# A second buffer for the S5 input matrix, filled one chunk ahead, in a hybrid decoder trunk

## The chip, the cores and the metric

The kernel runs on one core of a Trainium2 chip. The metric is the device time of one execution in microseconds (us); lower is better. The engines are named as in the profile: PE (TensorE, matrix products), PEld (its weight loads), DVE (VectorE), ACT (ScalarE), POOL (GpSimd) and SP (SyncE, which here only issues transfers). Each engine works through its own list of instructions, and waits on semaphores for the others.

## The reference, cut to what matters

Two layers (DEPTH = 2) over 288 columns: one prompt of 256 positions and 8 samples of 4. Everything is float32.

```python
def _layer(x, ...):
    z = x @ w_in
    u, cv, cg = z[..., :1024], z[..., 1024:2048], z[..., 2048:]
    y5, h_re, h_im = _s5(u, h0_re, h0_im, ...)        # 64 groups x 16 channels, 64 complex states
    g5 = gelu(y5);  s5_out = g5 * sigmoid(g5 @ s5_w_glu)
    c = causal_dwconv(cv * sigmoid(cg), width 31);  c = silu(_ln(c))
    x = _ln(ALPHA * x + concat([s5_out, c]) @ w_out)
    ...                                               # ConvFFN and input embedding, each with an _ln

def _s5(u, ...):
    bu = einsum(u, q * B)              # into the states; q from lam and dt
    h  = associative_scan(a, bu)       # over positions
    y  = Re(C h) + d * u
```

The product into the states (`bu`) and the one out of them (`y`) are what the change is about; the rest of the layer is most of the time.

## The kernel before

The big projections run on PE over blocks of 128 x 128 weights with 288 columns. A weight arrives as `wraw` (eight blocks, 512 KB); ACT rounds it to `whi` (L202), DVE makes the remainder `wlo` (L145, a helper through which all DVE work goes), and PE multiplies three times per block (L379, L384 or L381, L385), so a unit of eight blocks is 24 matmuls. I count PE's place in the program in such matmuls from the start of the layer's input projection, and call this its position. The first blocks of layer 0 are multiplied in float32 at once (L375).

Beside the projections of a layer's mixer runs the S5 part, in 8 chunks of 128 channels (`c` = 0 to 7), written as Python generators that a small planner advances whenever PE has been given enough work. It keeps two accounts of time, `pe_t` for what PE and `dve_c` for what DVE has been given; `wait(ns)` and `until(t)` yield until `pe_t` has passed a time, `at(ns, fn)` calls `fn` then. So the planner only sets the order of instructions on each engine. For chunk c:

- `make_e`: the rows of B are scaled by q on DVE (`s5_into`: four instructions that read `sqb`, `sbt`; "into" below) and spread by two ACT instructions under two masks into the block-diagonal `em` (L947). In layer 1 the scaled rows are made early in layer 0's feed-forward, go to memory (`se_d`) and come back as `sbt`, so there is no "into".
- `make_o`: the matrix out of the states, `om`, and the short-range matrix: DVE makes `pw` and `bsm`, PE multiplies them (`kps`, L807), ACT copies the product under masks (`kp`, L812), DVE adds d, and through memory (`k_d`) it becomes `tm`.
- `inject`: PE makes `bu` from `em` and the chunk's columns `ust` (L399, 64 matmuls). It sets `state["i"] = c`.
- `scan`: DVE turns, scans and turns back the states and writes them shifted to `hin`. POOL makes the tables for it (`stb`, L990, finished on ACT at L996).
- `tail`: PE makes `y` from `hin` with `om` and `ust` with `tm` (L399), ACT and DVE apply the gelu.

`kps`, `y` and the set-up's `tp` share one PSUM buffer (tag "one"), so the `y` of chunk c, which stands behind the `kps` of chunk c + 1 in the program, needs that `kps` read out by `kp`. `em` has one buffer: chunk c + 1's may be written once chunk c's `bu` is done, and `prep`, which makes the matrices, waits for `state["i"] >= c - 1` first. The width-31 convolution of the mixer's other half (eight parts) gives `cvo`, eight tiles.

In the set-up of layer 0, `tp` (L710) transposes q through PE; POOL stores it (`q_d`, L717) and loads it spread out as the first `sqb` (L751).

Of the kernel before, what the change touches and what calls it, by code (L numbers as in the profile page):

```python
# [7 lines left out]
F32 = mybir.dt.float32  # L8
# [5 lines left out]
P = 128  # L14
# [5 lines left out]
TOK = SEQ + NB * NT  # L20
# [5 lines left out]
S5C = 8  # L26
CVC = 8
# [15 lines left out]
NCH = TOK // STEP  # L43
# [21 lines left out]
L0_LAG = 4000.0  # L65
LOOK = 1
FREE_LAG = 500.0
EARLY_LAG = 7000.0
EARLY_RATE = 0.5
EV_GAP = 10  # L70
# [88 lines left out]
class Core:  # L159
# [46 lines left out]
    def stream_lo(self, upto):  # L206
        upto = min(upto, self.nblk // SB - 1)
        while self.next_lo <= upto:
# [8 lines left out]
            self.next_lo += 1  # L217
            self.freed.append((s + RAW_BUFS, self.dve_c + FREE_LAG))

# [25 lines left out]
    def at(self, ns, fn):  # L245

        self.timed.append((self.pe_t + ns, fn))

    def run_timed(self, force=False):
        for x in list(self.timed):  # L250
# [333 lines left out]
    def setup(self, mp):  # L584
# [34 lines left out]
        p, s = exp_parts(ld, *w)  # L619
# [7 lines left out]
        thl, t1, t2, f = tl(), tl(), tl(), tl()  # L627
# [21 lines left out]
        p, s = exp_parts(x1, *w)  # L649
# [50 lines left out]
        yield None  # L700
        for _ in range(W1):
            yield None
        tp = self.ps.tile([P, 512], F32, tag="one", name="tp", bufs=1)
        for s in range(4):
            for i in range(2):
# [108 lines left out]
    def s5_early(self, l, pool):  # L814
# [20 lines left out]
        for c in range(S5C):  # L835
            bt, qb = [self.s5_load(l, c, pool, eng, w) for w in "bq"]
            cc, bc = self.s5_load(l, c, pool, eng, "o")
            yield 1.0
            yield from self.wait(EARLY_LAG)
            m = work([P, 4, 2, ST])  # L840
            yield from self.s5_into(m, bt, qb)
            ed, od, kd = [self.dp.tile(shp, F32, tag=f"{n}_d{c}", name=f"{n}_d{c}", bufs=1) for n, shp in (
                ("se", [P, 4, 2, ST]), ("so", [P, 4, 2, 4, CIN]), ("sk", [P, 7 * 2 * CIN]))]
            yield from self.wait(EARLY_LAG)
            eng.dma_start(ed, m)
# [14 lines left out]
    def s5(self, l, mp):  # L860
# [5 lines left out]
        def once(n, shp):  # L866
            return mp.tile(shp, F32, name=n, tag=n, bufs=1)
        fin = once("fin", [P, NPAIR, 2, 9])
        h0 = once("h0", [P, NPAIR, 2, NB])
        self.sm = {"e": once("em", [P, 4, 2, P]), "o": once("om", [P, 4, 2, P])}  # L870
        em, om = self.sm["e"], self.sm["o"]
        tm = once("tm", [P, 4, P])
        pw = once("pw", [P, 4, 2, 5, CIN])
        bs = once("bsm", [P, 4, 2, 2, CIN])
# [49 lines left out]
        def load_o(c, eng):  # L924
            if early:
                o = mp.tile([P, 4, 2, 4, CIN], F32, name="sqb", tag="sqb", bufs=1)
                eng.dma_start(o, early[c][1])
                load_t(c, early[c][2])
                return (o,)
            return self.s5_load(l, c, mp, eng, "o")  # L930
# [8 lines left out]
        def make_e(c, bt, qb=None):  # L939
            m = bt  # L940
            if not early:
                m = work([P, 4, 2, ST])
                yield from self.s5_into(m, bt, qb)
            mf = m.rearrange("p q i s -> p (q i) s")
            ef = em.rearrange("p q i m -> p (q i) m")
            for g in range(2):
                nc.scalar.activation(ef[:, :, g * ST:(g + 1) * ST], mf, AF.Copy, scale=self.mask2[:, g:g + 1])  # L947

        def make_o(c, cc, bc=None):

            if early:
                pk = cc
            else:
                yield from self.s5_out(l, c, cc, bc, pw, bs, work)
                yield from self.wait(PJ_LAG)
                while state["y"]:
                    yield None
                state["k"] = True
                self.s5_steps(bs, pw, kp)
                self.at(PS_LAG + 500.0, lambda: state.update(k=False))  # L960
                yield None
                k0 = kp[:, 3].rearrange("p g o -> p (g o)")
                V.scalar_tensor_tensor(k0, self.eye, self.prm("s5_d", c), k0, op0=OP.mult, op1=OP.add)
                kd = self.dp.tile([P, 7 * 2 * CIN], F32, tag="k_d", name="k_d", bufs=2)
                G.dma_start(kd, kp.rearrange("p k g o -> p (k g o)"))
                pk = pw[:, :, :, 1:5]
            while state["p"] < c - 1:
                yield None
            of = om.rearrange("p q i (r g o) -> p (q i) r g o", g=2, o=CIN)
            pf = pk.rearrange("p q i k o -> p (q i) k o")  # L970
            for g in range(2):
                h = slice(g * ST, (g + 1) * ST)
                nc.scalar.activation(of[h, :, :, g], pf[h], AF.Copy)
            if early:
                self.at(PS_LAG, lambda: state.update(o=c))
                return

            def back():
                load_t(c, kd)
                self.at(LOAD_LAG, lambda: state.update(o=c))  # L980
            self.at(BACK_LAG, back)
# [14 lines left out]
            self.at(2500.0, lambda: nc.scalar.activation(f, tb, AF.Sin, scale=6.283185307179586 / 4294967296.0))  # L996
            return f

        def inject(us):
            v = self.ps.tile([P, 2, 512], F32, tag="two", name="bu", bufs=1)  # L1000
            self.pe_t += 1000.0
            for q in range(4):
                for i in range(2):
                    self.strips(v[:, i, q * NCH:(q + 1) * NCH], em[:, q, i], us[:, q], True, True)
            return v

        def scan(c, v, tb):
# [69 lines left out]
        state = {"i": -1, "p": -1, "e": -1, "o": -1, "y": False, "k": False}  # L1077
        finals = []

        def prep():  # L1080
            if l == 0:
                yield from self.wait(Q_LAG)
            while l and not self.u_d:
                yield None
            ge = load_e(0, nc.gpsimd, bt0)
            yield from self.wait(L0_LAG if l == 0 else LOAD_LAG)
            go = go0
            for c in range(S5C):
                while state["i"] < c - 1:
                    yield None  # L1090
                yield from make_e(c, *ge)
                state["e"] = c
                if c + 1 < S5C:
                    self.at(B_LAG, lambda: nxt.append(load_e(c + 1, nc.sync)))
                yield from make_o(c, *go)
                if c + 1 < S5C:
                    go = load_o(c + 1, nc.sync)
                    while not nxt:
                        yield None
                    ge = nxt.pop()  # L1100
                    yield from self.wait(3000.0)
            self.rate = RATE[l]

        def main():
            if l == 0:
                yield from self.wait(M0_LAG)
            G.memset(om, 0.0)
            tb = tables(0)
            initial()
            for c in range(S5C):  # L1110
                while c not in ready or state["e"] < c:
                    yield None
                self.rate = RATE[l]
                v = inject(us[c])
                state["i"] = c
                yield from self.wait(PS_LAG)
                yield from scan(c, v, tb)
                if c + 1 < S5C:
                    tb = tables(c + 1)
                streams.insert(0, tail(c, us.pop(c)))  # L1120
# [21 lines left out]
        nxt = []  # L1142
# [10 lines left out]
        us, ready = {}, set()  # L1153
# [5 lines left out]
    def mixer(self, l, ph):  # L1159
        nc, a = self.nc, self.a  # L1160
        V = self.V
        with self.tc.tile_pool(name="mx", bufs=1) as mp:
            self.u32 = [mp.tile([P, TOK], F32, name=f"u32_{c}", tag=f"u32_{c}") for c in range(S5C)]
            cvo = [mp.tile([P, TOK], F32, name=f"cvo_{c}", tag=f"cvo_{c}") for c in range(CVC)]
            self.u_d, self.gdone = {}, []
            scan = self.scan = self.start(self.s5(l, mp), 0.0)

# [472 lines left out]
```

## Time and profile before

| | us |
|---|---|
| three runs | 2725.92, 2732.58, 2732.72 (median 2732.58) |
| profiled execution | 2730.52, span 2728.7, mean granted clock 0.99 |
| busy in the span | PE 2661.9, DVE 1836.0, ACT 1353.4, POOL 331.7 |

The span runs from the first to the last instruction of the profiled execution; times in the views count from its start. Layer 0's mixer lies at about 28 to 275 us, layer 1's at about 1376 to 1640 us. In a row of the timeline the bracket gives how long the engine sat idle before that instruction, and what it waited for.

### The profile page before, as it was taken

To read this page: it belongs to the slowest core of one execution; us is meant where nothing else is said; L and a number is where in the kernel's file an instruction comes from. 1 tells how busy PE (TensorE), PEld (TensorE's weight loads), DVE (VectorE), ACT (ScalarE), POOL (GpSimd) and SP (SyncE) were. 2 spreads that over 40 slices of the span, in tenths; PEclk is the share of its full clock that TensorE was granted. 3 is DMA by queue.
4 is the path that set the end of the run, shared out by engine and by line. 5 is a ranking of instruction groups with operands and counts; after the bars stand their busy time and mean duration, and the time that the engine had idled before them with its cause. 6 is when DMAs were issued, how large, how long until landed. Compare 5 with 4: busy or idle time off the path is not lost.

```text
span 2728.7 us, 57971 instructions
## 1 busy us (share of the span) xinstructions
PE 2661.9 (98%) x23696; PEld 2603.1 (95%) x23696; DVE 1836.0 (67%) x3016; ACT 1353.4 (50%) x2224; POOL 331.7 (12%) x913
## 2 busy tenths in 40 slices
PE   8889999999999999999998999999999999999997
PEld 7888999999999999999988889999999999999997
DVE  6986767665677556667776668776546664566686
ACT  3444547553555345546464445565435553455363
POOL 3553001000001000000034420010000000000000
PEclk9999999999999999999999999999999999999998
DMA  7877544555566645554568764454545555455543
GB/s 239 241 229 224 167 151 158 169 190 190 183 197 199 200 155 170 172 167 153 165 193 236 224 196 166 158 161 157 189 159 164 161 185 167 159 162 182 163 150 102
DMA packets 188041, 487.99 MB, mean 179 GB/s; under 512 B 48416, under 2 KB 74288, under 8 KB 187520
## 3 DMA queue, kind: packets, MB, share of 16 engines
q1 hardware_dynamic: 176896, 444.27, 51.0%
q0 software_dynamic: 10880, 40.03, 5.2%
q8 instruction: 186, 3.05, 0.5%
q14 instruction: 79, 0.65, 0.1%
HBM read 463.98 MB, written 24.87 MB: 179 GB/s over the span
## 4 chain that ended last, share of the span: by engine, by line
PE 88%; DVE 3%; DMA 3%; issue 1%; ACT 1%; POOL 1%; SPq 0%; ACTq 0%; DVEq 0%; POOLq 0%
PE acc L379 28%; PE acc L384 26%; PE acc L385 26%; PE acc L361 2%; PE acc L381 2%; PE acc L1225 2%; DVE sw L145 1%; PE y L399 1%; DMA cbuf<-in_convi_dram 1%; DVE wlo L145 1%; DMA ust<-u_d 1%; DVE x L145 1%; PE bu L399 0%; PE lnp L469 0%; DMA sqb<-q_d 0%
## 5 line engine op out<-in xcount | busy, mean ns | idle before, releaser
L379 PE MATMUL acc<-xh,whi 128*128 128x288 f32 x4656 | 1378.7, 296 | 7.6 <-ACT e L1344 3.2
L385 PE MATMUL acc<-xh,wlo 128*128 128x288 f32 x4357 | 1287.7, 296 | 3.0 <-issue 3.0
L384 PE MATMUL acc<-xl,whi 128*128 128x288 f32 x4357 | 1289.0, 296 | 0.6 <-DVE xl L145 0.3
L202 ACT ACTIVATE whi<-wraw 128x1024 fp32r<-128x1024 f32 x766 | 791.6, 1051 | 331.8 <-PE acc L384 211.2
L145 DVE TENSOR_TENSOR wlo<-wraw,whi 128x1024 fp32r<-128x1024 f32 x766 | 922.9, 1227 | 31.8 <-ACT whi L202 14.3
L379 PEld LDWEIGHTS acc<-xh,whi 128*128 128x128 f32 x4656 | 879.3, 189 | 15.4 <-ACT e L1344 4.1
L385 PEld LDWEIGHTS acc<-xh,wlo 128*128 128x128 f32 x4357 | 821.8, 189 | 3.3 <-issue 3.3
L384 PEld LDWEIGHTS acc<-xl,whi 128*128 128x128 f32 x4357 | 821.9, 189 | 2.4 <-DVE xl L145 2.0
L379 PE MATMUL acc<-hh,whi 128*128 128x288 f32 x1408 | 416.3, 296 | 0.0
L145 DVE SCALAR_TENSOR_TENSOR fo<-fe,parf,fo 128x304 f32<-128x304 f32 x352 | 188.3, 535 | 323.3 <-ACT fo L1377 317.0
L385 PE MATMUL acc<-hh,wlo 128*128 128x288 f32 x1312 | 387.7, 296 | 0.0
L384 PE MATMUL acc<-hl,whi 128*128 128x288 f32 x1312 | 387.0, 295 | 0.0
L379 PEld LDWEIGHTS acc<-hh,whi 128*128 128x128 f32 x1408 | 265.1, 188 | 0.5
L384 PEld LDWEIGHTS acc<-hl,whi 128*128 128x128 f32 x1312 | 247.0, 188 | 0.0
L385 PEld LDWEIGHTS acc<-hh,wlo 128*128 128x128 f32 x1312 | 246.7, 188 | 0.0
L1373 ACT ACTIVATE fe<-acc 128x256 f32<-128x256 f32 x176 | 67.6, 384 | 287.8 <-PE acc L385 287.8
L1383 POOL COPY fstage<-fe 128x9 f32<-128x9 f32 x176 | 45.0, 256 | 1037.0 <-ACT fe L1374 1014.1
L438 ACT ACTIVATE ln_q<-x 128x288 f32<-128x288 f32 x90 | 40.2, 446 | 221.5 <-DVE x L145 221.5
L145 DVE TENSOR_TENSOR x<-x,acc 128x288 f32<-128x288 f32 x64 | 29.1, 454 | 139.3 <-PE acc L385 139.3
L1377 ACT ACTIVATE fo<-fe,parf 128x304 f32<-128x304 f32 x176 | 113.1, 643 | 16.4
L1397 ACT ACTIVATE hh<-fth 128x288 fp32r<-128x288 f32 x88 | 39.2, 446 | 163.2 <-DVE fth L145 163.2
L145 DVE SCALAR_TENSOR_TENSOR x<-x,acc 128x288 f32<-128x288 f32 x64 | 29.0, 453 | 123.8 <-PE acc L385 123.7
(251 smaller groups left out, 2389.4 us busy)
## 6 DMA issues: line engine op xcount, KB each, us to landing
wraw<-in_wts_dram SPq DMA_DIRECT2D x776, 512.0 KB
stack<-cb_d POOLq DMA_DIRECT2D x32, 282.0 KB, 6.6
big<-cb_d POOLq DMA_DIRECT2D x24, 282.0 KB, 6.7
cbuf<-in_convi_dram POOLq DMA_DIRECT2D x16, 283.5 KB, 7.3
cb_d<-cbuf POOLq DMA_DIRECT2D x16, 283.5 KB, 3.6
out_dram<-cb_d POOLq DMA_DIRECT2D x16, 283.5 KB, 8.0
sbt<-in_s5b_dram SPq DMA_DIRECT2D x15, 256.0 KB
sqb<-q_d SPq DMA_DIRECT2D x60, 64.0 KB
```

The lines of the kernel that those rows point to most:

```text
L145: return f(out, *args, **kw)
L202: self.nc.scalar.activation(hi, self.raw[s], AF.Copy)
L361: nc.tensor.matmul(out, w, xl, start=False, stop=False)
L379: nc.tensor.matmul(out, w[0], xh, start=first, stop=False)
L381: nc.tensor.matmul(out, w[1], xh, start=False, stop=False)
L384: nc.tensor.matmul(out, w[0], xl, start=False, stop=False)
L385: nc.tensor.matmul(out, w[1], xh, start=False, stop=last)
L438: nc.scalar.activation(st["q"], v, AF.Square)
L1225: nc.tensor.matmul(o[32 * b:32 * b + 32, :SEQ], cw[:, b, k], st[:, b, 4 * k:4 * k + SEQ], start=(k == 0), stop=False, tile_position=(0, 32 ...
L1373: nc.scalar.activation(e[:, 2:2 + SEQ], acc[:, :SEQ], AF.Copy)
L1377: nc.scalar.activation(o[:, :w], e[:, 2:EW], AF.Identity, bias=self.prm("ffn_conv_b", m), scale=self.prm("ffn_conv_w2", m))
L1383: nc.gpsimd.tensor_copy(stage[:, z, :, 0], e[:, SEQ:EW:6])
```

## The change

`em` gets a second buffer, `em2`, which takes the place of the last four conv outputs (they become one tile `cv4`, of which `em2` uses the first 1024 columns; conv output 4 is written after chunk 7's `bu`). Even chunks use `em`, odd ones `em2`. `prep` makes chunk c + 1's `em` interleaved with chunk c's `make_o`, and waits only for `state["i"] >= c - 2`. A chunk's `bu` is now put into the program only when both accounts are past the making of its `em` by E_LAG (1500 ns in layer 0, 3500 in layer 1). And `tp` waits until PE's account has passed DVE's by 1500 ns.

```diff
+E_LAG = (1500.0, 3500.0)
+    def done(self, ns):
+        return max(self.pe_t, self.dve_c) + ns
...
+        yield from self.until(self.dve_c + 1500.0)
         tp = self.ps.tile([P, 512], F32, tag="one", name="tp", bufs=1)
...
+        ems = [em, self.em2]
...
-            ef = em.rearrange("p q i m -> p (q i) m")
+            ef = ems[c % 2].rearrange("p q i m -> p (q i) m")
...
-                    self.strips(v[:, i, q * NCH:(q + 1) * NCH], em[:, q, i], us[:, q], True, True)
+                    self.strips(v[:, i, q * NCH:(q + 1) * NCH], ems[c % 2][:, q, i], us[:, q], True, True)
...
-            for c in range(S5C):
-                while state["i"] < c - 1:
+            def into(c, ge):
+                while state["i"] < c - 2:
                     yield None
                 yield from make_e(c, *ge)
-                state["e"] = c
+                self.timed.append((self.done(E_LAG[l]), lambda c=c: state.update(e=c)))
                 if c + 1 < S5C:
                     self.at(B_LAG, lambda: nxt.append(load_e(c + 1, nc.sync)))
-                yield from make_o(c, *go)
+            def next_e(c):
+                while not nxt:
+                    yield None
+                yield from self.wait(3000.0)
+                yield from into(c, nxt.pop())
+            yield from into(0, ge)
+            for c in range(S5C):
+                out = make_o(c, *go)
                 if c + 1 < S5C:
+                    yield from self.among([out, next_e(c + 1)])
                     go = load_o(c + 1, nc.sync)
-                    while not nxt:
-                        yield None
-                    ge = nxt.pop()
                     yield from self.wait(3000.0)
+                else:
+                    yield from out
...
+            cv4 = mp.tile([P, half * TOK], F32, name="cv4", tag="cv4")
+            cvo += [cv4[:, c * TOK:(c + 1) * TOK] for c in range(half)]
+            self.em2 = cv4[:, :8 * P].rearrange("p (q i m) -> p q i m", q=4, i=2)
```

Every engine keeps the same set of instructions; their order moves, in the two mixers alone. On PE, `bu` 0 and 1 of layer 0 stay at positions 374 and 440; `kps` 0 moves from 320 to 374, `kps` 1 from 446 to 476, and `y` 0 from 488 to 494. In layer 1 `bu` 0 to 4 move 12 matmuls later.

On ACT, in layer 0, before (line numbers of the kernel before): `kp` here is chunk 1's, `em` chunk 2's.

```order
L812 ACTIVATE kp_212<-kps_871,mask2_166 128x4x16 x2
L996 ACTIVATE stb_827<-stb_827 128x576
L1247 ACTIVATE cvt_915<-acc_782 128x288
...
L1055 ACTIVATE yw_1051<-y_969 128x288
...
L996 ACTIVATE stb_1033<-stb_1033 128x576
L1061 ACTIVATE yw_1051<-yw_1051 128x288
L947 ACTIVATE em_207<-sw_1086,mask2_166 128x8x64 x2
```

The same place now (lines shifted by 1 to 21): chunk 2's `em` stands ahead of chunk 1's `kp`.

```order
L1003 ACTIVATE stb_824<-stb_824 128x576
L954 ACTIVATE em_204<-sw_879,mask2_166 128x8x64 x2
L1268 ACTIVATE cvt_902<-acc_765 128x288
L203 ACTIVATE whi_917<-wraw_763 128x1024
L818 ACTIVATE kp_209<-kps_938,mask2_166 128x4x16 x2
L203 ACTIVATE whi_967<-wraw_822 128x1024
```

`em` moved past `kp`, so `kp` has ahead of it an instruction that waits for chunk 2's "into" on DVE.

On DVE, layer 0, before: `sw_896<-bu_832` begins chunk 1's scan, `sw_1086<-sqb_805` chunk 2's "into", which stands behind the whole scan.

```order
L145 TENSOR_TENSOR wlo_823<-wraw_627,whi_774 128x1024
L145 SCALAR_TENSOR_TENSOR kp_212<-eye_124,par_173,kp_212 128x32
L145 TENSOR_TENSOR sw_896<-bu_832,stb_827 128x576
...
L145 TENSOR_TENSOR hin_213<-sw_896,sw_897 128x4x63
L145 TENSOR_TENSOR wlo_1075<-wraw_825,whi_963 128x1024
L145 TENSOR_TENSOR yw_1051<-yw_1051,y5_1050 128x288
L145 TENSOR_TENSOR sw_1086<-sqb_805,sbt_803 128x512
```

Now, from chunk 1's `bsm` on (`sw_892<-bu_829` begins chunk 1's scan):

```order
L146 TENSOR_TENSOR bsm_208<-sw_782,sw_783 64x4x16 x4
L146 TENSOR_TENSOR sw_711<-sw_711,stb_542 128x576
L146 TENSOR_TENSOR hin_210<-sw_712,sw_711 128x4x63
L146 TENSOR_TENSOR hin_210<-sw_711,sw_712 128x4x63
L146 TENSOR_TENSOR wlo_820<-wraw_621,whi_759 128x1024
L146 TENSOR_TENSOR sw_879<-sqb_802,sbt_800 128x512
L146 TENSOR_TENSOR sqb_802<-sqb_802,sbt_800 128x512
L146 TENSOR_TENSOR sw_879<-sw_879,sqb_802 128x4x64 x2
L146 TENSOR_TENSOR sw_892<-bu_829,stb_824 128x576
```

Chunk 2's "into" moved ahead of chunk 1's scan; chunk 0's scan now ends behind chunk 1's `bsm`.

On POOL, in layer 0's set-up, before (`u_d` are the stores of the first four chunks' columns, `cbuf` a load for the convolution):

```order
L717 DMA q_d<-em 256x1x128 x2
L751 DMA sqb<-q_d 128x1x128 x4
L1172 DMA u_d_448<-u_0_178 128x288
...
L1236 DMA cbuf<-in_convi_dram 128x567
L1107 MEMSET om 128x1024
```

And now:

```order
L723 DMA q_d<-em 256x1x128 x2
L1193 DMA u_d_440<-u_0_178 128x288
...
L1257 DMA cbuf<-in_convi_dram 128x567
L757 DMA sqb<-q_d 128x1x128 x4
L1123 MEMSET om 128x1024
```

The first `sqb` load moved behind the four stores and the `cbuf` load.

## Rows read from the trace of the kernel before

**Rows 1.** The page, busy time of engines and their share of the span.
```profile
PE 2661.9 (98%) x23696; PEld 2603.1 (95%) x23696; DVE 1836.0 (67%) x3016; ACT 1353.4 (50%) x2224; POOL 331.7 (12%) x913
```

**Rows 2.** Waits on PE: us in total, times, longest.
```profile
PE bu L399 <- ACT em L947: 7.9, 8, 3.0
```

**Rows 3.** Timeline of PE, layer 0: start, us, instruction, idle before and releaser.
```profile
58.15 1.21 PE L399 MATMUL bu<-ust,em 128*32 128x72 f32 x64 [0.27 <-DMA ust<-u_d]
...
69.90 1.21 PE L399 MATMUL bu<-ust,em 128*32 128x72 f32 x64 [1.62 <-DMA tm<-k_d]
...
72.03 0.43 PE L807 MATMUL kps<-pw,bsm 128*32 128x64 f32 x16
...
85.59 0.61 PE L381 MATMUL acc<-xh,wlo 128*128 128x288 f32 x1 [2.23 <-DVE wlo L145]
...
95.02 0.32 PE L399 MATMUL bu<-ust,em 128*32 128x72 f32 x4 [3.04 <-ACT em L947]
...
137.38 1.65 PE L399 MATMUL bu<-ust,em 128*32 128x72 f32 x64 [0.76 <-DMA ust<-u_d]
...
151.43 0.47 PE L399 MATMUL y<-ust,tm 128*32 128x72 f32 x8 [3.88 <-ACT kp L812]
```

**Rows 4.** Timeline of PE, layer 1.
```profile
1461.01 0.41 PE L399 MATMUL bu<-ust,em 128*32 128x72 f32 x4 [2.66 <-ACT em L947]
...
1529.97 2.15 PE L399 MATMUL bu<-ust,em 128*32 128x72 f32 x64 [3.11 <-DMA ust<-u_d]
```

**Rows 5.** Stretches: length, busy PE, PEld, DVE, ACT, POOL; granted clock, DMA share, GB/s.
```profile
85.50:90.00 4.50, 4.41 (x22) 4.41 (x23) 4.46 (x8) 1.33 (x3) 1.67 (x3) 0.62 0.89 241
...
96.00:99.00 3.00, 3.00 (x61) 2.80 (x52) 2.68 (x5) 0.82 (x1) 1.62 (x5) 0.50 1.04 262
151.40:156.00 4.60, 4.57 (x102) 4.37 (x103) 1.90 (x5) 1.36 (x3) 2.20 (x4) 0.50 1.03 242
...
1461.00:1464.00 3.00, 2.79 (x65) 2.33 (x66) 2.53 (x4) 2.20 (x3) 2.92 (x4) 0.52 0.80 270
60.00:215.00 155.00, 139.28 (x2414) 126.64 (x2415) 140.10 (x227) 72.30 (x136) 79.65 (x128) 0.96 0.83 237
```

**Rows 6.** Timeline of DVE, layer 0: "into", `make_o` (63.91 to 67.47), a split, the end of a scan.
```profile
40.99 0.69 DVE L145 TENSOR_TENSOR sw<-sqb,sbt 128x512 f32<-128x512 f32 x1 [7.58 <-issue]
...
59.14 0.68 DVE L145 TENSOR_TENSOR sw<-sqb,sbt 128x512 f32<-128x512 f32 x1
59.86 0.69 DVE L145 TENSOR_TENSOR sqb<-sqb,sbt 128x512 f32<-128x512 f32 x1
60.59 0.76 DVE L145 TENSOR_TENSOR sw<-sw,sqb 128x256 f32<-128x256 f32 x2
63.91 1.29 DVE L145 TENSOR_TENSOR sw<-scc,aP 128x512 f32<-128x512 f32 x2 [2.56 <-DMA scc<-in_s5c_dram]
65.12 1.22 DVE L145 TENSOR_TENSOR wlo<-wraw,whi 128x1024 fp32r<-128x1024 f32 x1
...
67.47 0.79 DVE L145 TENSOR_TENSOR bsm<-sw 64x64 f32<-64x64 f32 x4
68.27 1.42 DVE L145 TENSOR_TENSOR sw<-bu,stb 128x576 f32<-128x576 f32 x2
...
74.64 1.22 DVE L145 TENSOR_TENSOR hin<-sw 128x252 f32<-128x252 f32 x2
```

**Rows 7.** Timeline of ACT, both layers.
```profile
72.58 0.52 ACT L812 ACTIVATE kp<-kps,mask 128x64 f32<-128x64 f32 x2 [1.71 <-PE kps L807]
...
78.93 1.06 ACT L202 ACTIVATE whi<-wraw 128x1024 fp32r<-128x1024 f32 x1 [1.52 <-DMA wraw<-in_wts_dram]
...
94.27 1.32 ACT L947 ACTIVATE em<-sw,mask 128x512 f32<-128x512 f32 x2
...
1460.23 1.33 ACT L947 ACTIVATE em<-sbt,mask 128x512 f32<-128x512 f32 x2 [1.67 <-DMA sbt<-se_d]
```

**Rows 8.** Timeline of POOL, layer 0's set-up.
```profile
36.30 2.42 POOL L751 DMA_DIRECT2D sqb<-q_d  x4 [2.46 <-DMA q_d<-em]
...
45.97 0.54 POOL L1236 DMA_DIRECT2D cbuf<-in_convi_dram  x1
```

More of the change, by code (lines that the diff above doesn't have):

```diff
@@ L997, in tables, with inject @@
             return f
-        def inject(us):
+        def inject(c, us):
             v = self.ps.tile([P, 2, 512], F32, tag="two", name="bu", bufs=1)
@@ L1113, in main @@
                 self.rate = RATE[l]
-                v = inject(us[c])
+                v = inject(c, us[c])
                 state["i"] = c
@@ L1163, in mixer @@
             self.u32 = [mp.tile([P, TOK], F32, name=f"u32_{c}", tag=f"u32_{c}") for c in range(S5C)]
-            cvo = [mp.tile([P, TOK], F32, name=f"cvo_{c}", tag=f"cvo_{c}") for c in range(CVC)]
+            half = CVC // 2
+            cvo = [mp.tile([P, TOK], F32, name=f"cvo_{c}", tag=f"cvo_{c}") for c in range(half)]
+            cv4 = mp.tile([P, half * TOK], F32, name="cv4", tag="cv4")
+            cvo += [cv4[:, c * TOK:(c + 1) * TOK] for c in range(half)]
+            self.em2 = cv4[:, :8 * P].rearrange("p (q i m) -> p q i m", q=4, i=2)
             self.u_d, self.gdone = {}, []
```

## The prediction

> **What bounds the kernel now.** I read the page first: PE is busy for 2661.9 of 2728.7 us, so only what PE waits for, or does slowly, can be won [rows 1]. The list of PE's waits then says how much of that concerns this change: `bu` waits for `em` on ACT eight times, 7.9 us together [rows 2]. PE's timeline places them and their neighbours: in layer 0, `bu` 1 waits 1.62 us for a load, a product waits 2.23 us for a late remainder `wlo`, `bu` 2 waits 3.04 us for `em`, and `y` 3 waits 3.88 us for `kp` [rows 3]; in layer 1, 2.66 us at `bu` 3 is the longest one for `em` [rows 4]. The stretches show what comes behind such a wait: the granted clock is 0.62 over 4.5 us after the late remainder, 0.50 over 3 us after `bu` 2 and over 4.6 us after `y` 3, and 0.52 over 3 us after the 2.66 us in layer 1 [rows 5]. 0.50 is the 1.2 GHz level. Of a stretch at 0.62, (1 - 0.62) x 2 x 4.5 = 3.4 us are at half speed, and a microsecond there does half of its work. So the three spells of layer 0 hold 3.4 + 3.0 + 4.6 = 11.0 us at half speed, 5.5 us lost; the one in layer 1 holds 2.9 us, 1.4 lost.
>
> The last thing to see is that DVE stands as near its limit as PE in layer 0's mixer: from 60 to 215 us DVE is busy for 140.10 of 155 us and PE for 139.28 [rows 5]. Putting DVE's instructions in another order there makes one thing earlier by making another later. That is the heart of this case.
>
> **Layer 0, the start.** `tp` moves later, and the first `sqb` load now stands on POOL behind the `u_d` stores and `cbuf`, so it starts at 45.97 + 0.54 = 46.5 instead of 36.30 [rows 8]. Before, the first "into" started 40.99 - 36.30 = 4.7 us after the load did [rows 6, 8]; now it starts at about 51.2. "Into" takes 2.2 us (59.14 to 60.59 + 0.76), a split 1.2, `make_o` on DVE 3.2 (63.91 to 67.47 + 0.79, less the split inside) [rows 6], so `bsm` 0 is ready at 57.8. `kps` 0 has moved to just ahead of `bu` 0, whose place PE reached at 58.15 - 0.27 = 57.9 [rows 3]. The 10 us are thus just covered: I count 0, and if the load were 3 us later than this, it would cost 3.
>
> **bu 1.** From the end of `bu` 0 to PE's arrival at `bu` 1 (69.90 - 1.62) are 8.9 us for 66 matmuls, so a position is 0.135 us [rows 3]. The `ust` loads of the first two chunks go ahead of chunk 1's `sbt` and `sqb` on SP's queue, so I take the 1.62 us as gone; the other end is that it stays. PE then has `bu` 1 at 68.3.
>
> **y 0: the new wait.** `kps` 1 now stands at position 476 and `y` 0 at 494, with 18 x 0.135 = 2.4 us between, and `y` 0 needs `kp` 1. On ACT `kp` 1 has `em` 2 ahead of it, which waits for chunk 2's "into" on DVE. DVE's list from `bsm` 0 (57.8): two splits 2.4, "into" of chunk 1 2.2, some small ones 0.9, so 63.3; then chunk 0's scan 6.4 (68.27 to 74.64 + 1.22, less a split) [rows 6], `make_o` of chunk 1 3.2, three splits 3.6, "into" of chunk 2 2.2: 78.7. On ACT follow `em` 1.32, a `whi` 1.06 and `kp` 0.52 [rows 7]: 81.6. PE comes to `y` 0 at 68.3 + 1.2 + 36 x 0.135 + 0.43 + 2.4 = 77.2. So `y` 0 waits 4.4 us, and I expect the clock to fall behind it as behind the waits above: 1.7 us more (3.4 at half speed).
>
> Here a rule speaks against the change. The Trainium skill says, in "PSUM — Partial Sum Buffer", section "Engine vs sequencer instructions", that the queues of ScalarE and VectorE are strictly first in, first out. By it every `kp` is held as long as the `em` ahead of it; this is the first rival below. The trace bears it out in layer 0: `y` 3's 3.88 us came from a `kp` that stood behind other ACT work.
>
> **The late remainder (2.23)** is gone: its split stands shortly behind chunk 2's "into", at about 82, while PE, held at `y` 0, needs it some 2.7 us later than before (85.59 - 2.23), at 86.0. **bu 2 (3.04)** is gone: `em` 2 is ready at about 80, PE comes at 93 or later. **y 3 (3.88)** is gone: `kp` 4 now stands ahead of the conv output and its square on ACT, and part 1 of the convolution stands between `kps` 4 and `y` 3 on PE. With these three their spells at half speed go: 5.5.
>
> **What comes back later in layer 0.** `y` 1, 2, 4 and 5 also stand only 18 to 24 matmuls behind a `kps`, with `kp` behind `em`. Each may wait between 0 and the 6.1 us of `y` 0 with its clock. A chunk asks of DVE "into" 2.2, `make_o` 3.2, scan 6.4, five splits 6.1 and a few small ones, some 19 us; of PE 114 positions, 15.4, and its own products, 18 to 19. It is a close race, which DVE loses a little: I take 1.5 us each, 6 in all. `bu` 4 waited 0.76 us for `ust` [rows 3]; PE comes earlier there, while the load follows other traffic on SP: 1 more.
>
> Layer 0: -1.6 + 4.4 + 1.7 - 2.2 - 3.0 - 3.9 - 5.5 + 6 + 1 = -3.1.
>
> **Layer 1** has no "into", and DVE is not its limit. `em` waited for its `sbt` (1.67 us at chunk 3 [rows 7]), `bu` for `em`. Made a chunk ahead, some 19 us, both are covered; if a load came later than that, ACT would be held, with the `whi` behind it. Of the 7.9 us, 4.9 lie behind `bu` 2 of layer 0, nearly all here: -4.9, and -1.4 for the clock. `bu` 0 to 4 come 12 matmuls, 1.6 us, later; the scan behind them is not waited for at once. The 3.11 us that `bu` 6 waits for `ust` [rows 4] stays, since that load stands behind the same stores. For waits that form anew I give back 1.5, between 0 and 3. Layer 1: -4.8.
>
> The new wait on the accounts and the one ahead of `tp` are only in the planner, and put no instruction on the chip. Work on each engine is unchanged.
>
> **Sum.** -3.1 - 4.8 = -7.9 on the profiled execution's 2730.52: 2722.6. The median of the runs shown is 2 us higher, their lowest 5 us lower.
>
> **Rivals.**
> First, slower: the `kp` behind `em` holds all of `y` 1, 2, 4 and 5 as it holds `y` 0. Then the 6 us are 4 x 6.1 = 24.4, and the sum is +10.5: 2741. It decides from the second such `y` on: two at 6.1 and two at 1.5 make 15.2, and the sum is +1.3. For it speaks DVE's 90% of busy time; against it that `y` 0 has the late start against it, which later chunks don't.
> Second, everything goes through: no new wait in layer 0. The sum loses 4.4 + 1.7 + 6 + 1 more: -21, 2709.5. Against it stands that DVE was idle for only 14.9 us of the 155, so layer 0 can't give 16 without a DVE that never waits. I hold 2711 for its end.
> Third, no change: the two-buffered `em` removes its own waits, but DVE's arrears turn up at the next splits and `y`, and layer 1's at `ust` and the tables. Layer 0 gives 0 and layer 1 two to four: about 2728.
>
> **How the numbers follow.** My forecast 0.45 (its own range 2714 to 2729), first rival 0.15, second 0.12, third 0.28. A measurement of this kernel tells about 0.3%, 8 us, from no change. Faster by more: the second rival, and 0.30 of the 0.45: 0.42. Slower by more: the first rival, 0.14 of it. The rest, 0.44, lies within. The range 2711 to 2737 leaves out the ends of the first and second rival.
>
> **What would show it.** In the new profile: `bu` no longer waits for `em` in either layer; `y` 0 at about 77 us waits some 4 us for `kp`, with the clock at 0.5 behind it; the wait on `wlo` near 85 us and that of `y` 3 are missing; the first "into" starts near 51 us. I am wrong if `y` 0 does not wait, if three or more of the later `y` wait over 3 us, or if the start costs PE more than 2 us ahead of `bu` 0.

## The result, and the profile after

The changed kernel takes 2751.4 us (median of 6 runs, 2746.9 to 2754.3) against 2732.65 (6 runs, 2725.9 to 2735.5) of the kernel before on the same chip: ratio 1.0073, 95% interval 1.0062 to 1.0084. It is slower, and outside my range. The first rival had the direction, not the size: 2741. One execution of number 9 below (10741.5 us) and one of number 12 (3231.2 us) are far above the rest and are left out of every median and ratio.

The profiled execution took 2754.3 us, its span is 2752.5, 23.8 longer than before. I divide it at two marks that both traces have. One is the product behind `ln_s` that ends the mixer of a layer, the other the `lnp` sums that end layer 0.

| | before | after | |
|---|---|---|---|
| end of layer 0's mixer | 288.95 | 307.90 | +18.9 |
| from there to the end of layer 0 | 1078.74 | 1078.73 | 0 |
| layer 1 up to the end of its mixer | 270.40 | 275.22 | +4.8 |

The middle part is the same to 0.5 us in every kernel of this study, so the two ends can be compared by themselves.

The list of PE's waits in the kernel after (us in total, times, longest) answers to [rows 2]:

```profile
PE y L404 <- ACT kp L818: 14.9, 4, 5.2
PE bu L404 <- issue: 8.7, 3, 5.3
...
PE bu L404 <- DMA ust<-u_d: 7.3, 2, 4.5
...
PE acc L386 <- DVE wlo L146: 4.8, 3, 1.6
PE bu L404 <- DMA sqb<-q_d: 3.7, 1, 3.7
...
PE kps L813 <- DVE bsm L146: 2.5, 2, 2.3
...
PE bu L404 <- ACT cv L954: 0.8, 1, 0.8
```

The second buffer (its tile is called `cv`) does what it says: `bu` waits 0.8 us for its matrix where it waited 7.9. But 14.9 us of `y` waiting for `kp` are new, and more for `ust`, `wlo` and `bsm`. The timeline of PE in layer 0, after, answers to [rows 3]:

```profile
61.24 0.66 PE L813 MATMUL kps<-pw,bsm 128*32 128x64 f32 x16 [2.26 <-DVE bsm L146]
...
75.08 1.21 PE L404 MATMUL bu<-ust,cv 128*32 128x72 f32 x64 [0.78 <-ACT cv L954]
...
93.05 0.47 PE L404 MATMUL y<-ust,tm 128*32 128x72 f32 x8 [5.25 <-ACT kp L818]
...
115.77 0.33 PE L404 MATMUL y<-ust,tm 128*32 128x72 f32 x8 [2.20 <-ACT kp L818]
137.76 0.33 PE L404 MATMUL y<-ust,tm 128*32 128x72 f32 x8 [3.09 <-ACT kp L818]
...
203.59 0.36 PE L404 MATMUL y<-ust,tm 128*32 128x72 f32 x8 [4.36 <-ACT kp L818]
```

`kps` 0 waits 2.26 us for `bsm` 0; `y` 0 waits 5.25, at 93 and not at 82; `y` 1, 2 and 5 wait 2.2, 3.1 and 4.4; `bu` 2 and `y` 3 wait for nothing. The stretches of the kernel after answer to [rows 5] (length, busy PE, PEld, DVE, ACT, POOL; granted clock, DMA share, GB/s):

```profile
62.00:66.00 4.00, 4.00 (x72) 3.80 (x62) 2.23 (x5) 1.61 (x4) 0.64 (x1) 0.50 0.54 165
93.00:97.00 4.00, 3.95 (x100) 3.75 (x101) 3.93 (x7) 1.65 (x3) 1.27 (x3) 0.50 0.66 213
...
60.00:215.00 155.00, 131.09 (x2148) 120.27 (x2149) 135.19 (x223) 70.13 (x136) 76.56 (x124) 0.91 0.77 221
```

The clock is at 0.50 behind `kps` 0 and behind `y` 0. From 60 to 215 us DVE, the engine with no time to spare, is busy 4.9 us less than before, and PE 8.2 us less. From 28 us to the end of layer 0's mixer PE is idle for 30.4 us and was for 18.1; that is 12.3 of the 18.9 (`y` waiting for `kp` makes 11.0 of it, 14.9 for 3.9). Its busy time went from 242.8 to 249.4 for the same products: 6.6 more, the price of the lower clock.

Where DVE lost its time stands in its own timeline, after, which answers to [rows 6]:

```profile
53.88 0.76 DVE L146 TENSOR_TENSOR sw<-sqb,sbt 128x512 f32<-128x512 f32 x1 [4.89 <-DMA sqb<-q_d]
...
63.98 0.25 DVE L146 SCALAR_TENSOR_TENSOR kp<-eye,par,kp 128x32 f32<-128x32 f32 x1
71.32 0.69 DVE L146 TENSOR_TENSOR sw<-sqb,sbt 128x512 f32<-128x512 f32 x1 [7.09 <-DMA sqb<-q_d]
...
73.46 1.41 DVE L146 TENSOR_TENSOR sw<-bu,stb 128x576 f32<-128x576 f32 x2
...
86.88 1.15 DVE L146 TENSOR_TENSOR sw<-sqb,sbt 128x512 f32<-128x512 f32 x1
...
89.90 1.41 DVE L146 TENSOR_TENSOR sw<-bu,stb 128x576 f32<-128x576 f32 x2
```

The first "into" starts at 53.88. Then DVE stands still for 7.09 us ahead of chunk 1's "into", with chunk 0's scan (the `sw<-bu` at 73.46), whose `bu` has been there for nearly ten us, behind it. Its load is late on SP (transfers in the order of issue, after):

```profile
50.38 7.01 SPq L943 DMA_DIRECT2D ust<-u_d  x8
58.03 4.88 SPq L187 DMA_DIRECT2D wraw<-in_wts_dram  x2
62.99 0.38 SPq L750 DMA_DIRECT2D sbt<-in_s5b_dram  x1
63.57 2.60 SPq L757 DMA_DIRECT2D sqb<-q_d  x4
```

ACT's timeline after, which answers to [rows 7], shows how the lateness reaches `y` 0:

```profile
73.58 1.34 ACT L954 ACTIVATE cv<-sw,mask 128x512 f32<-128x512 f32 x2 [9.94 <-DVE sw L146]
...
90.01 1.33 ACT L954 ACTIVATE em<-sw,mask 128x512 f32<-128x512 f32 x2 [3.43 <-DVE sw L146]
91.26 0.39 ACT L1268 ACTIVATE cvt<-acc 128x288 f32<-128x288 f32 x1
91.55 1.04 ACT L203 ACTIVATE whi<-wraw 128x1024 fp32r<-128x1024 f32 x1
92.49 0.50 ACT L818 ACTIVATE kp<-kps,mask 128x64 f32<-128x64 f32 x2
```

`em` of chunk 2 waits for DVE, `kp` of chunk 1 stands behind it, and 0.6 us after `kp` began `y` 0 starts.

### The profile page after: what moved, and what is told of

The parts are those of the page before. It is cut to its first block, busy times and chain, and to the rows that moved or that the text cites. A ratio compares the mean times of both kernels' runs of the same rounds, so it can differ in the third digit from the quotient of the medians.

```text
span 2752.5 us, 57968 instructions
## 1 busy us (share of the span) xinstructions
PE 2668.6 (97%) x23696; PEld 2608.5 (95%) x23696; DVE 1833.6 (67%) x3016; ACT 1353.1 (49%) x2224; POOL 336.4 (12%) x913
## 4 chain that ended last, share of the span: by engine, by line
PE 88%; DVE 5%; DMA 4%; ACT 2%; issue 1%; SPq 1%; POOL 0%; ACTq 0%; DVEq 0%
PE acc L384 27%; PE acc L389 26%; PE acc L390 26%; PE acc L366 2%; PE acc L386 2%; PE acc L1246 2%; PE acc L380 2%; DMA wraw<-in_wts_dram 1%; DVE sw L146 1%; DVE wlo L146 1%; DMA sbt<-se_d 1%; PE y L404 1%; DMA scc<-in_s5c_dram 1%; DVE x L146 1%; PE lnp L474 0%
## 5 line engine op out<-in xcount | busy, mean ns | idle before, releaser
L1398 ACT ACTIVATE fo<-fe,parf 128x304 f32<-128x304 f32 x176 | 113.0, 642 | 16.7 <-ACT fe L1395 0.4
```

Source lines behind the costliest of these rows:

```text
L1398: nc.scalar.activation(o[:, :w], e[:, 2:EW], AF.Identity, bias=self.prm("ffn_conv_b", m), scale=self.prm("ffn_conv_w2", m))
```

## The experiments

After the result I held that layer 0's loss has three causes in a row on DVE: the late start (`tp` and the first `sqb` load), chunk 1's "into" ahead of chunk 0's scan with its load not there yet, and `kp` behind `em` on ACT. The rivals: one of the three is the whole of it; or the second buffer and the wait on the accounts cost by themselves. Times are medians; the ratio is to the kernel before on the same chip. "Layer 0" is the end of its mixer and "layer 1" the length up to the end of its mixer, both of the one profiled execution, where before has 288.9 and 270.4. Such a length carries the difference of single executions: kernels whose edits leave a layer alone lie up to 7 us apart there (layer 1 takes 269.8 us in number 11 and 276.4 in number 7, 275.3 in number 1). So the 4.8 us that layer 1 is longer in the table above are within that spread, and what a layer costs is read from the medians.

**1. The buffer alone, in the kernel before** (nothing made earlier).

```diff
-            ef = em.rearrange("p q i m -> p (q i) m")
+            ef = ems[c % 2].rearrange("p q i m -> p (q i) m")
```

> The kernel before with the second em buffer alone: em alternates between the two places, the planner's order and waits untouched. Theory: em is late by DVE's 'into' and by the loads, not by the buffer, so bu still waits for em for 6 to 8 us in all, and the time is 2730 to 2735. Rival: the single buffer is what held em; then bu's waits fall under 3 us and the time to 2722 to 2728.

2734.2 us, ratio 1.0001 (0.9991 to 1.0011). The place that it takes costs nothing, and a second buffer that nobody fills early brings nothing.

**2. The wait of `tp` alone, in the kernel before.**

```diff
+        yield from self.until(self.dve_c + 1500.0)
         tp = self.ps.tile([P, 512], F32, tag="one", name="tp", bufs=1)
```

> The kernel before, with only the wait of tp on DVE's account added. Theory S (the late start): the S5 chain of layer 0 starts some 10 us later and costs about 8 to 12 us, 2741 to 2745, although no kp stands behind an em. Rival K (kp queued behind em): nothing of the loss comes from tp, 2730 to 2736.

2734.5 us, ratio 1.0002 (0.9993 to 1.0012). Layer 0 is 5 us longer in its profile (293.9), with `kps` 0 waiting 2.26 us as in the changed kernel, but the medians don't show it.

**3. The changed kernel without the wait of `tp`.**

```diff
-        yield from self.until(self.dve_c + 1500.0)
```

> The changed kernel without the wait of tp; two em buffers, made a chunk ahead, as in the change. Theory S: 10 to 15 us better than the changed kernel, 2736 to 2741, and the first y waits under 1.5 us. Rival K: only 2 to 4 us better, 2747 to 2749, and three or more y still wait 2 to 5 us each for kp.

2751.4 us, ratio 1.0061 (1.0046 to 1.0076): as slow as with it. The first "into" is at 40.35 us and chunk 1's at 56.14, but now chunk 2's load is late: DVE waits 6.78 us for its `sqb` at 79.93, and `y`, which waits only 1.4 us for `kp`, waits 14.8 for `tm`. The late start is not the whole of it.

**4. The changed kernel with `E_LAG` at zero.**

```diff
-E_LAG = (1500.0, 3500.0)
+E_LAG = (0.0, 0.0)
```

> The changed kernel with E_LAG of 0 in both layers. If the wait of bu on the accounts costs or saves nothing: within 3 us of the changed kernel, 2748 to 2754. If it holds off waits of bu for em: 2756 or more, with bu waiting for em again. If it is itself a cost: below 2746.

2745.9 us, ratio 1.0048 (1.0033 to 1.0063). By the medians the wait on the accounts costs 5 to 6 us, though the two intervals just touch, and in which layer can't be told (layer 1 has 270.5 in place of 275.2, within the spread). It is not the main part: layer 0 still ends at 306.2, with `y` waiting five times for `kp`, 16.7 us.

**5. and 6. The change in one layer alone.** Number 5 is layer 0 alone: it has the new `prep` and the wait of `tp` there, and layer 1 as before. Number 6 is layer 1 alone: the new `prep` for `l == 1`, the old one and one buffer for layer 0, and `tp` as before. The lines shown are number 6's.

```diff
-            yield from into(0, ge)
...
+            if l == 1:
+                yield from into(0, ge)
...
+            else:
+                for c in range(S5C):
+                    while state["i"] < c - 1:
+                        yield None
...
```

> The change in layer 0 alone (with tp late); layer 1 made as before. If the parts add: 2746 to 2749, layer 0's mixer ending near 308 us. If layer 1 were the main loss it would be below 2740.

> The change in layer 1 alone: layer 0 and its set-up as before, one em buffer there. The changed kernel's layer 1 is about 5 us longer than before's. Theory L1 (the order of loads on SP in layer 1, which makes bu 5 wait for ust): 2737 to 2740, with bu 5 waiting 4 to 6 us for ust. Rival: layer 1 loses only because layer 0 hands it other states of the queues: 2728 to 2734.

Layer 0 alone 2748.1 us, ratio 1.0054 (1.0036 to 1.0072); layer 1 alone 2736.6, 1.0012 (1.0002 to 1.0022). So about 15 of the 19 us are layer 0's, and layer 1 costs 3 to 4 (the interval goes from 0.5 to 6) where I had counted a gain of 4.8.

**7. and 8. `kp` ahead of `em` on ACT**, in layer 0: a chunk's "into" waits until the `kp` of the chunk before is in the program. Number 8 also has `tp` without its wait.

```diff
                 yield from self.wait(3000.0)
+                while l == 0 and state["kc"] < c - 1:
+                    yield None
                 yield from into(c, nxt.pop())
```

> The changed kernel, but in layer 0 a chunk's em may only be put into the program once the kp of the chunk before is; tp as in the change. Theory S: 1 to 4 us better than the changed kernel, 2747 to 2750, because the chain still starts late. Rival K: the 14.9 us of y waiting for kp go, with their clock, 14 to 19 us better, 2732 to 2737.

> The changed kernel with both undone: no wait of tp, and em behind the kp of the chunk before. If S and K together are the loss, it is at or below the kernel before: 2722 to 2733. If neither is (a third cause, in layer 1 or in the loads), it stays above 2740.

2751.0 us, ratio 1.0052 (1.0034 to 1.0070), and 2744.1, 1.0034 (1.0022 to 1.0047). In number 7 the waits of `y` for `kp` are all but gone (0.5 us left of 14.9), and the time is the same. The list of PE's waits of number 7, from 28 to 250 us, says why:

```profile
PE kps L813 <- DVE bsm L146: 8.9, 6, 2.3
PE y L404 <- DMA tm<-k_d: 7.0, 2, 4.5
PE acc L386 <- DVE wlo L146: 4.1, 3, 1.6
PE acc L390 <- DVE wlo L146: 2.4, 2, 1.2
```

PE waits for the same late DVE at other places, since chunk 1's "into" still stands ahead of the scan and waits 7.18 us for its load. `kp` behind `em` was the place at which the lateness showed, not its source. Number 8 is 7 us better and still 10 above the kernel before, so the order on ACT and `tp` together are not the whole of it.

**9. Chunk 1's load early**, on POOL right behind chunk 0's, into a place of its own (the first conv outputs). One edit that the reader needs:

```diff
             ge = load_e(0, nc.gpsimd, bt0)
+            if l == 0:
+                nxt.append(load_1(nc.gpsimd))
```

> The changed kernel, but chunk 1's sbt and sqb of layer 0 have a place of their own (in the first four conv outputs' columns) and are loaded on POOL right behind chunk 0's. 'Into' stays ahead of the scan, em ahead of kp. Theory Q, by the load: DVE's 7 us wait for sqb near 71 us goes and the time falls by 5 to 9 us, 2742 to 2746. Rival O (the order itself, with kp behind em, costs it all): y 0 still waits 4 or more us for kp, and the time falls by 0 to 3 us, 2748 to 2751.

2751.9 us, ratio 1.0067 (1.0047 to 1.0087). DVE's 7.09 us are gone: its timeline has the `sw<-cv` of chunk 1's "into" (the loads lie in `cv` now) right behind a split, and PE's `y` 0 hardly earlier.

```profile
64.79 0.69 DVE L146 TENSOR_TENSOR sw<-cv 128x512 f32<-128x512 f32 x1
```

```profile
90.96 0.47 PE L404 MATMUL y<-ust,tm 128*32 128x72 f32 x8 [6.76 <-DMA tm<-k_d]
```

Here `kps` 0 starts at 63.62 in place of 61.24, and `em` of chunk 1 stands ahead of `kp` of chunk 0 on ACT, which runs at 69.51 and not at 61.95; its store on POOL follows at 76.69 (73.25 in the changed kernel) and its way through memory (`tm`) holds `y` 0. Taking one of the causes away hands the wait to the next.

**10. and 11. One number: the wait ahead of a chunk's "into" in layer 0 from 3000 to 9000 ns**, which in number 10 puts chunk 1's "into" behind chunk 0's scan on DVE and its `em` behind `kp` on ACT, and gives the load 6 us more. Number 11 also has `tp` without its wait; there "into" (59.17) comes ahead of the scan (61.30), as in the kernel before (59.14 and 68.27).

```diff
-                yield from self.wait(3000.0)
+                yield from self.wait(9000.0 if l == 0 else 3000.0)
                 yield from into(c, nxt.pop())
```

> The changed kernel with one number changed: in layer 0 the next chunk's matrix is begun 9000 instead of 3000 ns after its load was put into the program. This puts 'into' back behind the scan on DVE, and kp ahead of em on ACT; tp stays late. Theory Q (DVE stands idle at an 'into' whose sqb has not landed, with the scan and the splits behind it): the 7 us wait of DVE for sqb near 71 us goes, 8 or more us better than the changed kernel, 2737 to 2743. Rival T (the late tp sets the start whatever follows): 2747 or more, layer 0's mixer still ending after 303 us.

> As the run with 'into' later, and tp without its wait: layer 0 then differs from before only in the second buffer and the later bu. Theory Q: layer 0's mixer ends at 285 to 292 us, and the time is 2730 to 2737, layer 1's loss being left. If the second buffer itself or the wait of bu on the accounts cost something: above 2740.

2742.4 us, ratio 1.0036 (1.0026 to 1.0047), and 2732.7, 1.0004 (0.9992 to 1.0016). The first takes 9 us back and the second all 19. The DVE timeline of number 10, at the place that had the 7.09 us:

```profile
64.19 0.24 DVE L146 SCALAR_TENSOR_TENSOR kp<-eye,par,kp 128x32 f32<-128x32 f32 x1
64.35 1.41 DVE L146 TENSOR_TENSOR sw<-bu,stb 128x576 f32<-128x576 f32 x2
...
72.46 0.68 DVE L146 TENSOR_TENSOR sw<-sqb,sbt 128x512 f32<-128x512 f32 x1
...
86.89 1.29 DVE L146 TENSOR_TENSOR sw<-scc,aP 128x512 f32<-128x512 f32 x2 [9.70 <-DMA scc<-in_s5c_dram]
```

The scan runs while the load is under way, and "into" finds it there. DVE doesn't idle less here, since it waits 9.70 us for another load at 86.89; but by then the scan and its `hin` are done, which in the changed kernel stand behind the wait. `kp` ahead of `em` and the longer time for the load come with the same edit, and numbers 7 and 9, which each had one of these alone, gained nothing; how the 9 us divide is not shown. `tp`'s wait costs 9.8 us between numbers 10 and 11 and nothing between the changed kernel and number 3, where a later load delays DVE in its place. But number 11 is only as fast as before. No `bu` waits for `em` in layer 0, and from 28 to 250 us `kps` waits 8.1 us for `bsm` and the products 5.1 for `wlo`: the saved waits came back at the next work of DVE.

**12. Layer 1 alone, with 9000 ns.** Number 6's kernel with the one number in layer 1.

```diff
-                yield from self.wait(3000.0)
+                yield from self.wait(9000.0)
                 yield from into(c, nxt.pop())
```

> The change in layer 1 alone, with the next chunk's matrix begun 9000 instead of 3000 ns after its load. Theory L1 (the order on SP that puts ust of chunk 5 behind other loads): the 7.9 us wait of bu 5 for ust goes, and bu does not wait for em; 2724 to 2730, below the kernel before. Rival: other waits take its place, 2730 to 2736.

2723.7 us, ratio 0.9966 (0.9952 to 0.9980): faster than both kernels. Layer 1 takes 259.5 us in place of 270.4 (270.4 to 275.3 over the four kernels that make it as before). Behind the layer norm at its start PE's only waits over 0.6 us there are "issue", 2.5 at most, with the granted clock at 1.00 from 1430 to 1580 us, where the changed kernel has 0.93 for most of it (its windows):

```profile
1430.00:1480.00 50.00, 42.08 (x623) 39.70 (x622) 30.23 (x40) 22.36 (x36) 22.28 (x37) 0.93 0.86 237
1480.00:1530.00 50.00, 44.63 (x918) 38.87 (x917) 35.36 (x47) 22.08 (x39) 27.46 (x45) 0.93 0.71 216
```

and the same of number 12:

```profile
1430.00:1480.00 50.00, 47.82 (x857) 44.03 (x857) 33.08 (x46) 25.72 (x44) 27.23 (x48) 1.00 0.95 268
1480.00:1530.00 50.00, 46.62 (x942) 41.98 (x944) 35.41 (x46) 26.50 (x44) 30.78 (x48) 1.00 0.84 248
```

What the short wait does in layer 1 is seen on two engines. ACT stands still at `em`, with the copies and `whi` behind it, because the load of `sbt` hasn't landed; its waits in the changed kernel, from 1376 to 1600 us (us in total, times, longest):

```profile
ACT em L954 <- DMA sbt<-se_d: 19.3, 3, 8.7
...
ACT cv L954 <- DMA sbt<-se_d: 5.8, 1, 5.8
```

That is 25.1 us; it was 7.9 in the kernel before and is 1.2 in number 12. And SP, in the changed kernel, ahead of the `ust` that `bu` 5 waits for:

```profile
1500.24 2.21 SPq L187 DMA_DIRECT2D wraw<-in_wts_dram  x3
1510.72 0.33 SPq L934 DMA_DIRECT2D sqb<-so_d  x1
...
1515.78 2.24 SPq L943 DMA_DIRECT2D ust<-u_d  x4
```

and on ACT at the same time:

```profile
1508.48 1.06 ACT L203 ACTIVATE whi<-wraw 128x1024 fp32r<-128x1024 f32 x1 [4.81 <-DMA wraw<-in_wts_dram]
1509.44 1.26 ACT L980 ACTIVATE om<-sqb 64x512 f32<-64x512 f32 x2
```

The load of the next chunk's out matrix has one buffer, `sqb`, and is asked for right behind the making of `em`. It must wait until the last one has landed and ACT has copied it to `om`; ACT waits for a weight. So SP's queue stands still from 1502.5 to 1510.7 (3.2 us for the landing, 5.0 for the copy), the `ust` loads come at 1515.8, and PE waits 4.51 us. The waits of SP for `om`, from 1376 to 1600 us (us in total, times, longest), in the changed kernel:

```profile
SPq L934 <- ACT om L980: 21.4, 5, 6.0
```

In the kernel before it was 14.1 us; in number 12 there is none. A long wait of SP for `om` need not cost time: it is 23.4 us in number 4, where `bu` waits only 1.3 us for `ust` and layer 1 takes the 270.5 us of before.

**13. That load later**, in number 6's kernel: the load of `sqb`, `pw` or `tm` is asked for 6000 ns later. The rule for `em` stays at 3000 ns, but the wait stands in the loop that makes both matrices, so the later `em` move too (chunk 5's from 1482.5 to 1494.4 us, in a layer that starts 2.1 us later).

```diff
                     yield from self.among([out, next_e(c + 1)])
+                    yield from self.wait(6000.0)
                     go = load_o(c + 1, nc.sync)
```

> Layer 1 alone as in the changed kernel (layer 0 and the set-up as before, the next chunk's matrix still made after 3000 ns), and only the load of the next chunk's out matrix (sqb, pw or tm) asked for 6000 ns later. Theory SP: layer 1 lost its time because that load waits on SP for ACT's copies of om, and holds SP's queue with ust of the next chunk behind it (SP waited 20.7 us for om; bu 5 then 7.9 us for ust). Then the wait of SP for om falls below 10 us, bu 5 no longer waits over 3 us for ust, and the time is 2724 to 2730. Rival E: the place of em on ACT is what costs; then it stays at 2734 to 2739, with the wait for ust still there or turned into one for wlo or for the tables.

2728.0 us, ratio 0.9985 (0.9976 to 0.9993). SP waits no more for `om`, `bu` 5 waits 1.29 us for `ust` (7.86 in number 6), and 8.6 us of the median are won against number 6 (7.4 by the ratios, since the chips differ). The forecast of theory SP came true, but ACT's waits for `sbt` at `em` went in the same run, from 27.0 us in number 6 to 3.4. So rival E, by which the place of `em` on ACT is what costs, is not excluded: the run took both waits away.

**14. The same load later in the kernel before**, with its one buffer.

```diff
                     self.at(B_LAG, lambda: nxt.append(load_e(c + 1, nc.sync)))
+                if l and c:
+                    go = load_o(c, nc.sync)
+                    yield from self.wait(4000.0)
                 yield from make_o(c, *go)
                 if c + 1 < S5C:
-                    go = load_o(c + 1, nc.sync)
+                    if l == 0:
+                        go = load_o(c + 1, nc.sync)
```

> The kernel before, with one buffer and its own order; in layer 1 alone the load of the out matrix (sqb, pw or tm) of a chunk is asked for behind the making of its em, and the making of om follows 4000 ns later. Theory SP alone: what layer 1 can win is the freeing of SP's queue (SP waited 14.1 us for om there before), and the second buffer is not needed for it: 2722 to 2727 us, ratio near 0.997, no wait of SP for om. Rival B: with one buffer em is still made just ahead of its product, so bu's waits for em in layer 1 (4.6 us, with the half speed behind them) stay and the load brings nothing by itself: 2730 to 2736.

2733.6 us, ratio 0.9996 (0.9987 to 1.0005): nothing, the size that the rival gave, though not by its way. SP's waits for `om` fell to 3.7 us, and `bu`'s for `em` in layer 1 to 1.2, but `bu` now waits 4.8 for `ust`. I read the gain of number 12 as that of the early matrix and of the freed queue together, since the buffer alone (number 1), the early matrix asked for too soon (number 6) and the freer queue with one buffer (number 14) give none. The three differ in the order of instructions too, so this is argued, not shown.

**15. Both layers at 9000 ns, `tp` without its wait.**

> The changed kernel with tp without its wait and with the wait ahead of the next chunk's matrix at 9000 instead of 3000 ns in both layers. If the two layers add up (each loses its own time for its own cause), layer 0 stays at its level of before (ratio 1.0004 alone, with layer 1 at 3000) and layer 1 goes from +4 to -9: about 2723 us, ratio 0.996 to 0.998. Rival: layer 0's best order only hands its arrears on, and the gain of layer 1 is partly its start at another place against the loads; then 2728 to 2733.

2728.55 us, ratio 0.9979 (0.9966 to 0.9991). Layer 1 has its whole gain (259.5), and layer 0 ends at 297.9, where number 11 had 293.4 and before 288.9. The median is above the expected 2723, which its rival had at 2728 to 2733. Number 12, which leaves layer 0 as it was, has the lowest ratio, but the two intervals overlap, so that the early matrix costs something in layer 0 even in the better order is not shown.

## Why the prediction was wrong

- **"The 10 us are thus just covered: I count 0."** This is the step that failed first. I let the first `sqb` load land 4.7 us after its issue, as before; on POOL it went at 44.59, where it was 36.30 before [rows 8] and 46.5 in my sum, and was used 9.3 us later, at 53.88 instead of 51.2. `kps` 0 waited 2.26 us and a product ahead of it 1.60 for `wlo`; more than 2 us ahead of `bu` 0 is what I had said would prove me wrong.
- **The list of DVE in "y 0: the new wait"** left out the load of chunk 1. I added up instructions (63.3 for the end of chunk 1's "into") and didn't ask when its `sbt` and `sqb` land: they stand on SP behind eight `ust` and two `wraw`, and "into" starts at 71.32. I had used that very order on SP in favour of `bu` 1, one part earlier. So DVE idles 7.09 us, with the scan behind it. `y` 0 waits 5.25, close to the 4.4, but at 93 us: PE comes to it 10.6 us later than the 77.2, having waited on the way for `bsm` and `wlo`. The wait that I had named was there; the lateness of all that stands behind chunk 1's "into" was not in the sum.
- **"The late remainder is gone"** was wrong in kind: one wait of 2.23 became 1.60, 1.60 and 1.20 [rows 3]. **"bu 2"** and **"y 3"** were right. `bu` 1 waits no more for a load, but 0.78 us for its matrix, where I had none. `bu` 4 did not wait, but `bu` 5 waited 3.75 us, where I had allowed 1 for such waits; the profile puts it down to an `sqb` load, which `bu` does not read.
- **"I take 1.5 us each, 6 in all"**: `y` 1, 2, 4 and 5 waited 2.2, 3.1, 0 and 4.4, together 9.7. The first rival asked for 24.4 and was wrong too: two waits over 3 us, not four. Its "two at 6.1" point was near; what it lacked was the loss at the start. Of the Trainium skill's rule ("PSUM — Partial Sum Buffer", "Engine vs sequencer instructions"), that ScalarE and VectorE take their queues strictly in order, the trace bears out both halves: `kp` 1 behind an `em` that waited 3.43 us for DVE (`y` 0 waited 5.25), and chunk 0's scan behind an "into" that waited 7.09. I weighed it for ACT and not for DVE.
- **Layer 1, "-4.9 em, -1.4 clock, +1.5 back"**: the `em` waits went as said and `bu` 6's wait for `ust` stayed (2.76 for 3.11); what came back in PE's idle time was 8.9 us in place of 1.5: 4.51 for `ust` at `bu` 5, behind SP's queue held by `sqb`, 1.6 for `wlo`, and 3.1 more of "issue". The step that failed is "made a chunk ahead, some 19 us, both are covered": a chunk ahead of its product is not 19 us behind its load. Of the four `em` that waited for `sbt`, ACT came to two at 4.0 and 4.9 us after the load was issued and to two before it was, and it stood there for 25.1 us. I had named this ("ACT would be held, with the `whi` behind it") and given it no price. Number 12, which asks for `em` 6000 ns later, has the gain: 9 us by the ratio. Which of the two held queues, ACT's or SP's, cost the time is not shown, since numbers 12 and 13 free both.
- **The clock, "-5.5" and "+1.7"**, in layer 0: the sum has 3.8 us less for work at the lower clock, and measured are 6.6 more. New waits came in the place of those that went, with the clock at 0.50 behind `kps` 0 and `y` 0, and the term is off by 10.4 us, nearly half of the layer's miss of 22.
- **Of the parts costed at nothing**, the buffer was rightly so (number 1); the wait on the accounts was not (some 5 us, number 4), nor was the one ahead of `tp` (9.8 us between numbers 10 and 11, though nothing in numbers 2 and 3).

The range failed because it held the new wait at `y` 0 as the one thing that DVE's order could cost. The profile after shows a chain: 12.3 us of PE's idle time and 6.6 of lower clock.

What stays open: whether layer 0 is longer with the matrix made early and in the better order; the single profiles say 4 to 9 us (numbers 11 and 15, with the same plan, differ by 4.5), the medians don't show it. And what PE's "issue" waits are; 5.32 us of them lie inside one `bu` in the changed kernel, 5.31 in number 13, and 0.5 at most in number 12. The traces point to PE's own instructions. The page of the profile lists a queue for them (transfers, MB, share):

```profile
q8 instruction: 186, 3.05, 0.5%
```

PE has 23696 products and as many weight loads, which is 255 for each of the 186 transfers. All 55 "issue" waits of 1 us or more in the two mixers, over the 17 traces, end 2.2 to 3.6 us after such a transfer (that of 5.32 us ends at 1473.1, the transfer is at 1470.4), while from 1400 to 1600 us of the kernel before there are 24 of them, one in 8 us. So the 3.1 us more of "issue" in layer 1 are most likely late instructions, which no run here tests.

## What to carry to other kernels

Making a thing one step ahead moves its input's load ahead too: before moving a consumer on an in-order engine, look up when the load lands, and what stands behind the consumer. Where an engine has no time to spare, a wait that is taken away at one place is handed to that engine's next consumer (numbers 3, 7 and 9 each removed one cause and gained nothing), so test causes in pairs. A load into a single buffer that is asked for too early holds the whole queue, and so does a consumer that is put on its engine before its load has landed. Here 6 us more between a load and its consumer made the difference in both layers: 9 us in layer 0 (number 10), and a loss of 3 to 4 turned into a gain of 9 in layer 1 (number 12).

## What the runs showed of the hardware that I had not expected

Small loads took very different times from issue to use: the four `sqb` transfers of a chunk took 4.7 us before, 9.3 on POOL behind the stores and `cbuf`, and (chunk 1's) 7.7 on SP behind `ust` and weights. And layer 1's mixer ran at a granted clock of 1.00 over 150 us in number 12, whose longest wait there is 2.5 us, where the kernel before had 0.93 from 1430 to 1480 us: of the 10.9 us between number 12 and the kernel before, PE's idle time is 5.3 (15.7 to 10.4) and its busy time 5.6 (254.7 to 249.1).
